# Gathers that keep their running row in two PSUM banks, and one comparison instruction for both one-hot tables of the gate build

## The chip, the cores and the metric

One core of a Trainium2 chip runs the whole program. The metric is the device time of one execution in microseconds (us), the median of three runs. Engines are named as the profile names them: PE (matrix products), PEld (its weight loads), DVE (VectorE), ACT (ScalarE), POOL (GpSimd), SP (the queue that issues most DMA transfers).

## The reference, cut to what matters

One layer: a mixer (an SSD scan and a dilated-window attention), a layer norm, then the PEER feed-forward block, for 1024 prompt tokens and 32 sample tokens of width 1024. Each token picks 128 of 16384 experts (8 heads, 16 each):

```
e = (take(i1, ci // 16) * 128 + take(i2, ci % 16))      # expert numbers
g = softmax(sc)                                         # gates
hid = gelu(einsum('thkd,td->thk', u_tab[e], xb))
out = einsum('thk,thkd->td', g * hid, v_tab[e])
y = layer_norm(ALPHA * h + out)
```

## The kernel before, in words

The prompt's first 512 tokens and the 32 sample tokens are **part 0**, the other 512 tokens **part 1**. Each part runs `first` (attention), `second` (convolutions, then the SSD scan beside the z projections), `third` (output product and norm) and `route` (choice of experts). Then `dense` follows. Stretches are named by these functions below; from 1250 us on all is part 1 or `dense`.

The feed-forward block is computed in two ways. For 608 tokens it is **dense**: all 128x128 experts are multiplied, in 16 chunks `c` of 8 hidden products (weights `in_ut`) and 8 output products (`in_vd`). The hidden rows are weighed with a dense table of gates `g`. For the other 448 tokens, the rows of the chosen experts are **gathered**: an indirect DMA on POOL (L1829) fetches 128 rows of 4 KB, then DVE either multiplies them with the token's row and sums (L1855, table u), or adds them, scaled, to a running sum (L1860, table v). These 896 gathers are a lane of small steps, pumped at a fixed rate per tick beside all other work from part 1's `first` on. The operand that all gathers of a group of tokens share (the token's row `gh`, or the sum `acc`) is in `at`. It lies in SBUF until `dense` sets `self.seat` to two PSUM banks (6 and 7) late in its first chunk; from then on it lies there.

The **gate build** (`gates`, run in ticks beside the first six dense products) makes the table `g`. For each group of four tokens, of which there are 152, it does this: `o2` is where the expert's low number equals a position (DVE, L1603), times the gate (POOL, L1604). `o1` is the same for the high number, in three groups of five on DVE (L1610), in the others on ACT (L1607, L1608). Four fp32 products on PE (L1617) then give the table of four tokens, which ACT moves to SBUF (L1627), and SP to DRAM (`gd`, L1629). Four pairs of buffers (OBUFS) let the comparisons run three groups ahead. `choose` and `experts` prepare the numbers of later tokens in the same ticks.

In `dense`, `product` multiplies one weight tile into a pair of banks (48 matmuls, L427; `double` does two at L1751), and `hidden`, `early` or `output` empty it. Weights `wraw` come in two halves of 256 KB two steps ahead; ACT makes the high part (L368), POOL or DVE the low part (L369). The table `g` is loaded by `table` on SP (L1670), half a chunk (1216 KB, pieces of 512 B) in one DMA.

All engines work their instructions off in program order, and ticks put the lanes' instructions between the matmuls of a product. [...] `proj` takes its output banks from `self.ring` in turn: three banks in part 1's `second`, `third` (last product) and `route`.

Of the kernel before, what the change touches and what calls it, by code (L numbers as in the profile page):

```python
# [7 lines left out]
F32 = mybir.dt.float32  # L8
# [17 lines left out]
NE = 128  # L26
# [25 lines left out]
C_HSEL = C_BM + 8  # L52
C_TSEL = C_HSEL + 8
C_IOTE = C_TSEL + 16
C_NIOTE = C_IOTE + NE
C_PAY = C_NIOTE + NE
C_N = C_PAY + NPAIR


# [5 lines left out]


TPC = [(0, (TE // 32 + 1) // 2 * 32), ((TE // 32 + 1) // 2 * 32, TE // 64 * 32)]

ROWS, LOOK = 6, 5

# [15 lines left out]
NLO = "vpvpvpvp"  # L86


EQ, O1, OBUFS, EARLY = 4, "vavav", 4, [8, 16, 24, 30, 34, 40]


def const_arrays():
# [17 lines left out]
    c[:, C_NIOTE:C_NIOTE + NE] = -np.arange(NE)[None, :]  # L110
    c[:, C_PAY:C_PAY + NPAIR] = (np.arange(NPAIR)[None, :] + 1) * PACK

    def logc(dist):
# [138 lines left out]
class Build:  # L252
# [40 lines left out]
    def run(self):  # L293
# [11 lines left out]
        self.one = cp.tile([128, 1], F32, name="one")  # L305
# [24 lines left out]
    def start(self):  # L330
        nc, t = self.nc, self.t
        load = [(self.cst, t["cst"]), (self.heads, t["heads"].unsqueeze(0).to_broadcast([128, 2, 24])),
                (self.convw, t["convw"]), (self.chans, t["chans"]), (self.keys, t["keys"])]
        self.xrp = self.open("xr", side="right")
        x = self.inputs(0)
        self.load(0, 0)
        next(x)
        self.load(0, 1)
        next(x)
        self.cast(0, 0)  # L340
        self.load(1, 0)
# [12 lines left out]
        nc.vector.memset(self.eps, EPS)  # L354
        nc.vector.memset(self.one, 1.0)
# [457 lines left out]
    def second(self, hf):  # L813

        nc, t, T, PT = self.nc, self.t, self.T, self.PT
        self.ring = [0, 1, 2]
        self.y = self.open(f"y{hf}").tile([128, 12, T], F32, name="y")
        zp, self.zs = self.open(f"z{hf}", 2), 2 if hf else 3
        sp = self.open(f"ss{hf}")
# [329 lines left out]
    def third(self, hf):  # L1149
# [64 lines left out]
        for k, h in WO:  # L1214
            pcs = cuts if (k, 1) in END else self.pcs
            if h == 0:
                b = [[3, 4, 5, 0, 1, 2, 3, 5], [4, 0, 2, 4, 0, 2, 4, 0]][np_ - 1][k]
                acc[k] = [self.P[:, (b + i) % 6, :n] for i, (_, n) in enumerate(pcs)]
            else:
                self.wait(lambda: self.done["mix"])  # L1220
# [328 lines left out]
    def experts(self, sp, table, m, out):  # L1549
# [6 lines left out]
        nc.vector.tensor_single_scalar(ej[:m, 1], ei[:m], NE - 1, op=ALU.bitwise_and)  # L1556
        yield
        nc.vector.tensor_copy(en[:m], ej[:m])
        nc.vector.tensor_scalar_mul(en[:m, 0], en[:m, 0], -1.0)
        yield  # L1560
        tp = self.bank(self.side())
        for k, src in enumerate((en[:m, 0], en[:m, 1], gf[:m])):
# [4 lines left out]
    def gates(self, sp):  # L1567
# [5 lines left out]
        given = 2  # L1573
        groups = [(w, t) for w in range(len(work)) for t in range(work[w][2], work[w][2] + work[w][0], 4)]
        eTs, o12, sts, outs, cp = dict(enumerate(self.given)), {}, {}, {}, {}

        def experts(w):

# [13 lines left out]
        def build(q):  # L1592
            if q >= len(groups):
                return
            w, t0 = groups[q]
            eT = eTs[w]
            o1 = sp.tile([128, 4, 128], F32, name="o1", tag="o1", bufs=OBUFS)
            o2 = sp.tile([128, 4, 128], F32, name="o2", tag="o2", bufs=OBUFS)

            def over(k):  # L1600
                return eT[:, k, t0:t0 + 4].unsqueeze(2).to_broadcast([128, 4, 128])

            nc.vector.tensor_tensor(o2, self.c(C_IOTE).unsqueeze(1).to_broadcast([128, 4, 128]), over(1), op=ALU.is_equal)  # L1603
            nc.gpsimd.tensor_tensor(o2, o2, over(2), op=ALU.mult)  # L1604
            if O1[q % len(O1)] == "a":
                for k in range(4):
                    nc.scalar.activation(o1[:, k], self.c(C_IOTE), AF.Abs, bias=eT[:, 0, t0 + k:t0 + k + 1])  # L1607
                nc.scalar.activation(o1, o1, AF.Relu, scale=-1.0, bias=self.one)  # L1608
            else:
                nc.vector.tensor_tensor(o1, self.c(C_NIOTE).unsqueeze(1).to_broadcast([128, 4, 128]), over(0), op=ALU.is_equal)  # L1610
            o12[q] = o1, o2

        def mults(q):
            o1, o2 = o12.pop(q)
            outs[q] = gp = self.bank(q % 3)
            for k in range(4):
                nc.tensor.matmul(gp[:, k * 128:(k + 1) * 128], o2[:, k], o1[:, k], start=True, stop=True)  # L1617

        def store(q):
            if q < 0:  # L1620
# [28 lines left out]
    def dense(self):  # L1649
# [11 lines left out]
        self.sides = [3]  # L1661

        def table(q):
            if q >= len(steps):
                return
            c, half, k = steps[q]
            if not half and k % 4 == 0:
                gs[c, k // 4] = g = dp.tile([128, n // 32, 4, 32], F32, name="g", tag="g", bufs=2)
                e0 = c * 8 + k
                nc.sync.dma_start(g, self.gd[:, :, e0:e0 + 4, :].rearrange("b j i t -> j b i t"))  # L1670

        def gelu(ge, ps):
            nc.scalar.activation(ge, ps, AF.Gelu)
# [93 lines left out]
        for k in range(8):  # L1767
            if k == len(EARLY):
                self.settle(table_lane)
                self.close("ga", "gc", "best")  # L1770
                dp = self.open("dn", 2)
                for q in range(8):
                    table(q)
            product(4 + k % 2 * 2, hs, EARLY[k] if k < len(EARLY) else DTICKS, lambda ps, k=k: early(k, ps))
        self.settle()
        for k in range(9):
            if k < 8:
# [4 lines left out]
        for q in range(8, 12):  # L1782
            table(q)
        for q, (c, half, k) in enumerate(steps[8:-LASTS], 8):
            table(q + 4)
            if half and k == 0:
                double(q % 3 * 2, (q + 1) % 3 * 2, (ah, al), 2 * DTICKS,
                       [lambda ps, c=c, k=k: output(c, k, ps) for k in range(2)])
            elif not half or k > 1:
                product(q % 3 * 2, (ah, al) if half else hs, DTICKS,  # L1790
                        lambda ps: (output if half else hidden)(c, k, ps))

            self.seat = self.bank(6, 2)

        q0 = self.q
        for i, (s, m) in enumerate(TPC):
            for j, (c, half, k) in enumerate(steps[-LASTS:]):
                ps = self.P[:, i + 2 * j, :m]
# [106 lines left out]
```

## Time and profile before

| | us |
|---|---|
| median of 3 runs | 3946.99 (3944.28 to 3955.53) |
| the profiled execution | 3943.13 |
| its span, first to last instruction | 3940.2 |
| PE busy | 3526.3 (89%) |
| DVE busy | 2826.4 (72%) |
| POOL busy | 2494.5 (63%) |
| ACT busy | 1381.6 (35%) |

The shares are means over stages that differ: the DVE stands near its limit in the middle of the program, PE in the last 1700 us. So the table says how much there is of each engine's work, not where the time is lost; for that the stretches have to be read apart.

### The profile page before, as it was taken

Reading aid. Unit: us, or ns where it says so; the run is one execution under the profiler, and the core shown is the slowest. Engines: PE = TensorE matmul, PEld = TensorE weight load, DVE = VectorE, ACT = ScalarE, POOL = GpSimd, SP = SyncE. Lnnn points to the kernel's source line nnn. Section 1 sums busy time; section 2 is a strip of 40 time slices with the busy share of each in tenths; the row PEclk is TensorE's granted clock in tenths of the full one; section 3 lists DMA queues with packets and bytes.
Section 4 is the critical chain, followed back from the end, with each engine's and each line's share of the span. In section 5 each row is a group of like instructions: output and inputs, shape, how many; then the busy total and the mean of one; then the engine's idle time right before and its main releaser. Section 6 shows DMA issues by size and latency. Waiting matters only on the chain.

```text
span 3940.2 us, 62009 instructions
## 1 busy us (share of the span) xinstructions
PE 3526.3 (89%) x22691; PEld 3178.6 (81%) x22691; DVE 2826.4 (72%) x5547; ACT 1381.6 (35%) x2651; POOL 2494.5 (63%) x2235
## 2 busy tenths in 40 slices
PE   7999898897997887895767999999999999999998
PEld 6757778895765555674666899999999999999997
DVE  2326644488779989899999767667766767776675
ACT  3423324343443333324778222222222222222223
POOL 3204554254747788645788677777767777776774
PEclk9999999998998998897778999999999999999999
DMA  5452235643546457522444789898988999998894
GB/s 159 127 164 74 75 128 199 211 156 107 155 158 212 152 161 249 195 73 78 158 158 185 258 314 324 314 339 316 335 309 318 327 319 339 329 324 304 309 320 154
DMA packets 385521, 875.40 MB, mean 222 GB/s; under 512 B 38976, under 2 KB 149952, under 8 KB 382272
## 3 DMA queue, kind: packets, MB, share of 16 engines
q0 software_dynamic: 129024, 469.82, 33.6%
q1 hardware_dynamic: 256192, 401.63, 30.6%
q8 instruction: 178, 2.92, 0.3%
q14 instruction: 127, 1.04, 0.1%
HBM read 805.40 MB, written 94.65 MB: 228 GB/s over the span
## 4 chain that ended last, share of the span: by engine, by line
PE 38%; DVE 12%; DMA 6%; issue 4%; POOL 3%; ACT 1%; SPq 0%; POOLq 0%; DVEq 0%; ACTq 0%
PE P L427 31%; PE P L1751 5%; DMA wraw<-in_ut 4%; DVE o L1603 2%; DVE acc L1860 2%; DVE o L1610 2%; POOL wlo L369 1%; POOL row L1829 1%; DVE row L1855 1%; POOL o L1604 1%; DMA lng<-in_ln 1%; PE P L1617 1%; DVE mr L1340 0%; PE P L1274 0%; DMA g<-gd 0%
## 5 line engine op out<-in xcount | busy, mean ns | idle before, releaser
L369 POOL TENSOR_TENSOR wlo<-wraw,whi 128x512 fp32r<-128x512 f32 (+1 forms) x621 | 818.2, 1324 | 652.7 <-ACT whi L368 620.5
L368 ACT ACTIVATE whi<-wraw 128x512 fp32r<-128x512 f32 (+1 forms) x820 | 494.8, 625 | 1318.2 <-PE P L427 485.9
L427 PE MATMUL P<-hh,whi 128*128 128x320 f32 (+3 forms) x2648 | 662.5, 315 | 35.9 <-DVE al L1683 27.4
L427 PE MATMUL P<-hh,wlo 128*128 128x320 f32 (+3 forms) x2648 | 655.9, 313 | 17.7 <-DVE wlo L369 9.5
L427 PE MATMUL P<-hl,whi 128*128 128x320 f32 (+3 forms) x2648 | 659.1, 313 | 3.5 <-POOL hl L1295 3.3
L1860 DVE SCALAR_TENSOR_TENSOR P<-row,hid,P 128x1024 f32<-128x1024 f32 x371 | 476.9, 1286 | 57.8 <-DMA row<-in_v,ecol 31.5
L1829 POOL DMA_INDIRECT row<-in_u,ecol x384 | 407.7, 1062 | 152.9 <-DVE row L1855 78.3
L427 PEld LDWEIGHTS P<-hh,whi 128*128 128x128 f32 x2648 | 452.2, 194 | 47.8 <-DVE al L1683 20.8
L427 PEld LDWEIGHTS P<-hh,wlo 128*128 128x128 f32 x2648 | 450.7, 193 | 28.0 <-DVE wlo L369 10.8
L1829 POOL DMA_INDIRECT row<-in_v,ecol x384 | 410.1, 1068 | 90.9 <-issue 71.5
L427 PE MATMUL P<-xh,whi 128*128 128x272 f32 (+4 forms) x1288 | 432.6, 346 | 32.9 <-ACT xh L368 17.3
L427 PEld LDWEIGHTS P<-hl,whi 128*128 128x128 f32 x2648 | 451.5, 193 | 12.8 <-POOL hl L1295 4.7
L1855 DVE SCALAR_TENSOR_TENSOR row<-row,P 128x1024 f32<-128x1024 f32 x320 | 381.8, 1215 | 102.6 <-DMA row<-in_u,ecol 74.0
L427 PE MATMUL P<-xl,whi 128*128 128x272 f32 (+4 forms) x1288 | 420.8, 337 | 7.6 <-POOL xl L369 6.6
L427 PE MATMUL P<-xh,wlo 128*128 128x272 f32 (+4 forms) x1288 | 418.0, 335 | 1.7 <-POOL wlo L369 1.7
L369 DVE TENSOR_TENSOR wlo<-wraw,whi 128x512 fp32r<-128x512 f32 (+1 forms) x199 | 222.7, 1119 | 212.4 <-ACT whi L368 188.3
L427 PE MATMUL P<-ah,wlo 128*128 128x320 f32 (+1 forms) x1536 | 341.9, 302 | 3.1 <-POOL wlo L369 3.1
L427 PE MATMUL P<-ah,whi 128*128 128x320 f32 (+1 forms) x1536 | 342.9, 302 | 0.0
L427 PE MATMUL P<-al,whi 128*128 128x320 f32 (+1 forms) x1536 | 341.4, 301 | 0.0
L1617 PE MATMUL P<-o,o 128*128 128x128 f32 x1216 | 219.2, 338 | 117.1 <-POOL o L1604 99.1
L1617 PEld LDWEIGHTS P<-o,o 128*128 128x128 f32 x1216 | 196.2, 243 | 141.0 <-POOL o L1604 133.6
L427 PEld LDWEIGHTS P<-xh,whi 128*128 128x128 f32 (+1 forms) x1288 | 246.8, 196 | 65.1 <-ACT xh L368 19.1
(393 smaller groups left out, 6794.1 us busy)
## 6 DMA issues: line engine op xcount, KB each, us to landing
wraw<-in_ut SPq DMA_DIRECT2D x256, 256.0 KB
wraw<-in_vd SPq DMA_DIRECT2D x256, 256.0 KB
wraw<-in_wt SPq DMA_DIRECT2D x176, 256.0 KB
gd<-gst SPq DMA_DIRECT2D x19, 2048.0 KB
g<-gd SPq DMA_DIRECT2D x32, 1216.0 KB
wraw<-in_wo SPq DMA_DIRECT2D x64, 256.0 KB
wraw<-in_wq SPq DMA_DIRECT2D x64, 256.0 KB
out_sk<-in_ck SPq DMA_DIRECT2D x8, 2040.0 KB
```

Of the source, the lines that this page charges most:

```text
L368: nc.scalar.activation(hi, src, AF.Copy)
L369: (eng or nc.vector).tensor_tensor(lo, src, hi.bitcast(F32), op=ALU.subtract)
L427: nc.tensor.matmul(outs[i], w[a][:, k, :m], x[b][k][:, s:s + n], start=first and st, stop=last and sp)
L1603: nc.vector.tensor_tensor(o2, self.c(C_IOTE).unsqueeze(1).to_broadcast([128, 4, 128]), over(1), op=ALU.is_equal)
L1604: nc.gpsimd.tensor_tensor(o2, o2, over(2), op=ALU.mult)
L1610: nc.vector.tensor_tensor(o1, self.c(C_NIOTE).unsqueeze(1).to_broadcast([128, 4, 128]), over(0), op=ALU.is_equal)
L1617: nc.tensor.matmul(gp[:, k * 128:(k + 1) * 128], o2[:, k], o1[:, k], start=True, stop=True)
L1751: nc.tensor.matmul(outs[i][j], self.ws[q0 + i][wi][:, e, :], x[xi][e][:, s:s + m], start=e == p == 0, stop=e == last and p == 2)
L1829: nc.gpsimd.indirect_dma_start(out=rows[k], out_offset=None, in_=t["uv"[tab]], in_offset=bass.IndirectOffsetOnAxis(ap=tables(gi)[0][:, s:s ...
L1855: nc.vector.scalar_tensor_tensor(r, r, 1.0, at, op0=ALU.mult, op1=ALU.mult, accum_out=hid[:, s:s + 1])
L1860: nc.vector.scalar_tensor_tensor(at, r, hid[:, s:s + 1], at, op0=ALU.mult, op1=ALU.add)
```

## The change

- From part 1's `second` on, `self.seat` is banks 2 and 3. The row or sum of the gathers moves there at the first gather in `second` and stays. `dense` no longer sets the seat.
- To free these banks, the ring has two banks instead of three, `third` takes its banks from 0, 1, 4 and 5, the dense products use the pairs 0, 4, 6 (`PAIRS`), the gate build's products the banks 0, 1, 7 and its transposes bank 6. The six early products all use pair 4, each emptied (`settle`, two more ticks) before the next.
- In the gate build, a copy of the numbers 0 to 127 (`iota`) is put into bank 6, and one DVE comparison of 1024 elements makes both tables `oo` of a group. ACT's share, the negated numbers and the constants for them go.
- `table` loads half a chunk of `g` in four pieces, one per output product of the chunk before, instead of at once four products ahead.

```diff
     def second(self, hf):
-        self.ring = [0, 1, 2]
+        self.ring = [0, 1] if hf else [0, 1, 2]
+        if hf:
+            self.seat = self.bank(2, 2)
...
-                b = [[3, 4, 5, 0, 1, 2, 3, 5], [4, 0, 2, 4, 0, 2, 4, 0]][np_ - 1][k]
+                b = [[0, 1, 4, 5, 0, 1, 4, 0], [4, 0, 2, 4, 0, 2, 4, 0]][np_ - 1][k]
...
-        nc.vector.tensor_scalar_mul(en[:m, 0], en[:m, 0], -1.0)
...
+        iota = self.bank(6)[:, 384:]
+        nc.scalar.activation(iota, self.c(C_IOTE), AF.Copy)
...
-            nc.vector.tensor_tensor(o2, self.c(C_IOTE).unsqueeze(1).to_broadcast([128, 4, 128]), over(1), op=ALU.is_equal)
-            nc.gpsimd.tensor_tensor(o2, o2, over(2), op=ALU.mult)
-            if O1[q % len(O1)] == "a":
-                for k in range(4):
-                    nc.scalar.activation(o1[:, k], self.c(C_IOTE), AF.Abs, bias=eT[:, 0, t0 + k:t0 + k + 1])
-                nc.scalar.activation(o1, o1, AF.Relu, scale=-1.0, bias=self.one)
-            else:
-                nc.vector.tensor_tensor(o1, self.c(C_NIOTE).unsqueeze(1).to_broadcast([128, 4, 128]), over(0), op=ALU.is_equal)
+            nc.vector.tensor_tensor(oo, iota.unsqueeze(1).unsqueeze(1).to_broadcast([128, 2, 4, 128]),
+                                    eT[:, 0:2, t0:t0 + 4].unsqueeze(3).to_broadcast([128, 2, 4, 128]), op=ALU.is_equal)
+            nc.gpsimd.tensor_tensor(oo[:, 1], oo[:, 1], eT[:, 2, t0:t0 + 4].unsqueeze(2).to_broadcast([128, 4, 128]), op=ALU.mult)
...
-            outs[q] = gp = self.bank(q % 3)
+            outs[q] = gp = self.bank([0, 1, 7][q % 3])
...
-                nc.sync.dma_start(g, self.gd[:, :, e0:e0 + 4, :].rearrange("b j i t -> j b i t"))
+                rows = slice(0, b) if part is None else slice(b * part // 4, b * (part + 1) // 4)
+                nc.sync.dma_start(gs[c, i][:, rows], self.gd[rows, :, e0:e0 + 4, :].rearrange("b j i t -> j b i t"))
...
-            product(4 + k % 2 * 2, hs, EARLY[k] if k < len(EARLY) else DTICKS, lambda ps, k=k: early(k, ps))
+            product(4 if k < len(EARLY) else PAIRS[k % 2 * 2 - 2], hs, EARLY[k] if k < len(EARLY) else DTICKS, lambda ps, k=k: early(k, ps))
+            if k < len(EARLY):
+                self.settle()
...
-            table(q + 4)
+            if half:
+                table(c + 1, k // 4, k % 4)
...
-            self.seat = self.bank(6, 2)
```

The first place is DVE's queue in the gate build, where the numbers of later tokens are prepared between the comparisons (`eT` holds a group's expert numbers, `cst` the constants). Before:

```order
L1603 TENSOR_TENSOR o_16470<-cst,eT 128x512
L1610 TENSOR_TENSOR o_16469<-cst,eT 128x512
L1860 SCALAR_TENSOR_TENSOR acc<-row,hid,acc 128x1024
L1528 CAST cf<-ci 128x256
L1529 CAST sf<-best_13986 128x128
L1530 TENSOR_SCALAR sf<-sf 128x128
L1603 TENSOR_TENSOR o_16489<-cst,eT 128x512
L1610 TENSOR_TENSOR o_16488<-cst,eT 128x512
L1539 TENSOR_TENSOR eq<-sf,cf 128x1024
```

and with the change:

```order
L1602 TENSOR_TENSOR oo<-P,eT 128x1024
L1854 SCALAR_TENSOR_TENSOR P<-row,hid,P 128x1024
L1529 CAST cf<-ci 128x256
L1530 CAST sf<-best_13984 128x128
L1531 TENSOR_SCALAR sf<-sf 128x128
L1602 TENSOR_TENSOR oo<-P,eT 128x1024
L1540 TENSOR_TENSOR eq<-sf,cf 128x1024
```

One instruction that reads PSUM stands where one or two that read SBUF twice stood, and the gather's sum is in `P`, the PSUM tile.

The second place is SP's queue in `dense`. Before, one chunk:

```order
L1670 DMA g<-gd 128x19x128
L395 DMA wraw<-in_ut 128x512 x8
L395 DMA wraw<-in_vd 128x512 x16
L1670 DMA g<-gd 128x19x128
L395 DMA wraw<-in_ut 128x512 x8
L1670 DMA g<-gd 128x19x128
```

and with the change:

```order
L393 DMA wraw<-in_ut 128x512 x10
L393 DMA wraw<-in_vd 128x512 x8
L1664 DMA g<-gd 128x4x128
L393 DMA wraw<-in_vd 128x512 x4
L1664 DMA g<-gd 128x5x128 x2
L393 DMA wraw<-in_vd 128x512 x2
L1664 DMA g<-gd 128x5x128
L393 DMA wraw<-in_vd 128x512 x2
```

The two large loads of a chunk have become eight small ones between the weights of the output products.

## Rows read from the trace of the kernel before

**Rows 1.** Page, part 4: the chain that ended last, by engine and line.
```profile
PE 38%; DVE 12%; DMA 6%; issue 4%; POOL 3%; ACT 1%; SPq 0%; POOLq 0%; DVEq 0%; ACTq 0%
```
**Rows 2.** Windows: us, then PE, PEld, DVE, ACT, POOL busy, clock, DMA share, GB/s.
```profile
1250.00:1540.00 290.00, 221.75 (x1067) 162.87 (x1068) 257.63 (x362) 102.35 (x195) 230.31 (x193) 0.91 0.54 173
1540.00:1660.00 120.00, 99.85 (x487) 83.09 (x485) 108.64 (x101) 35.37 (x64) 84.02 (x64) 0.90 0.69 238
...
1793.00:2172.00 379.00, 261.98 (x1514) 237.19 (x1515) 373.23 (x480) 269.57 (x472) 305.18 (x212) 0.80 0.41 151
...
2216.00:3913.00 1697.00, 1656.08 (x11742) 1651.47 (x11741) 1194.82 (x1482) 449.45 (x753) 1232.67 (x1118) 0.99 0.90 315
```
**Rows 3.** Lines of 1793 to 2172: busy us, mean ns, idle before, releasers.
```profile
L1604 POOL TENSOR_TENSOR o<-o,eT 128x512 f32<-128x512 f32 x152 | 210.6, 1395 | 88.1 <-DVE o L1603 85.3 <-DVE ei L1546 2.4
...
L1603 DVE TENSOR_TENSOR o<-cst,eT 128x512 f32<-128x512 f32 x152 | 151.6, 1019 | 0.8 <-ACT eT L1565 0.8
L1610 DVE TENSOR_TENSOR o<-cst,eT 128x512 f32<-128x512 f32 x91 | 105.5, 1160 | 0.0
...
L1860 DVE SCALAR_TENSOR_TENSOR acc<-row,hid,acc 128x1024 f32<-128x1024 f32 x31 | 67.2, 2167 | 0.0
```
**Rows 4.** Single lines, whole span: ns min/median/max, first and last start.
```profile
L1603 DVE TENSOR_TENSOR o<-cst,eT x152: 674/680/2847, 1793.0 to 2165.5; 128x512 f32<-128x512 f32 x152
L1604 POOL TENSOR_TENSOR o<-o,eT x152: 1032/1421/3162, 1793.8 to 2167.1; 128x512 f32<-128x512 f32 x152
L1860 DVE SCALAR_TENSOR_TENSOR P<-row,hid,P x371: 1273/1289/1292, 2212.7 to 3873.0; 128x1024 f32<-128x1024 f32 x186
L1860 DVE SCALAR_TENSOR_TENSOR acc<-row,hid,acc x77: 1270/2056/3393, 1535.8 to 2207.8; 128x1024 f32<-128x1024 f32 x77
L1677 DVE TENSOR_TENSOR P<-P,g x120: 783/794/800, 2263.4 to 3857.5; 128x608 f32<-128x608 f32 x120
L1855 DVE SCALAR_TENSOR_TENSOR row<-row,P x320: 1200/1216/1224, 2337.9 to 3726.9; 128x1024 f32<-128x1024 f32 x160
```
**Rows 5.** Lines of 1250 to 1540 (first row) and of 1540 to 1660 (second).
```profile
L1855 DVE SCALAR_TENSOR_TENSOR row<-row,gh 128x1024 f32<-128x1024 f32 x68 | 103.3, 1538 | 0.0
...
L1860 DVE SCALAR_TENSOR_TENSOR acc<-row,hid,acc 128x1024 f32<-128x1024 f32 x38 | 68.3, 1797 | 1.0 <-DMA row<-in_v,ecol 0.5
```
**Rows 6.** Timeline of `second`: DVE empties a bank; PE's next projection but one.
```profile
1415.23 0.68 DVE L1116 SCALAR_TENSOR_TENSOR z<-z,P 128x512 f32<-128x512 f32 x1
...
1424.10 0.48 PE L427 MATMUL P<-xh,whi 128*128 128x512 f32 x1
```
**Rows 7.** Chain in order of time: pairs of output products, by start and length.
```profile
2310.11 13.37 PE P L1751 x96
...
2752.37 13.37 PE P L1751 x96
...
2859.33 13.37 PE P L1751 x96
...
2977.67 13.37 PE P L1751 x96
...
3086.63 13.39 PE P L1751 x96
...
3855.20 13.38 PE P L1751 x96
```
**Rows 8.** Timeline of SP and of ACT, 3025 to 3062: start, length, instruction.
```profile
3035.98 0.43 SPq L1670 DMA_DIRECT2D g<-gd  x1
...
3055.73 0.63 ACT L368 ACTIVATE whi<-wraw 128x512 fp32r<-128x512 f32 x1 [11.54 <-DMA wraw<-in_ut]
```
**Rows 9.** A window behind that load, columns as in group 2.
```profile
3050.00:3055.00 5.00, 5.00 (x38) 5.00 (x37) 0.00 (x0) 0.00 (x0) 0.00 (x0) 1.00 1.04 401
```
**Rows 10.** DMA view of 2172 to 3941: queue, packets, MB, share; issues, KB each.
```profile
q1 hardware_dynamic: 153696, 180.78, 31.2%
...
g<-gd SPq DMA_DIRECT2D x32, 1216.0 KB
```

More of the change, by code (lines that the diff above doesn't have):

```diff
@@ L54 @@
 C_IOTE = C_TSEL + 16
-C_NIOTE = C_IOTE + NE
-C_PAY = C_NIOTE + NE
+C_PAY = C_IOTE + NE
 C_N = C_PAY + NPAIR
@@ L67 @@
 TPC = [(0, (TE // 32 + 1) // 2 * 32), ((TE // 32 + 1) // 2 * 32, TE // 64 * 32)]
+PAIRS = [0, 4, 6]
 ROWS, LOOK = 6, 5
@@ L86 @@
 NLO = "vpvpvpvp"
-EQ, O1, OBUFS, EARLY = 4, "vavav", 4, [8, 16, 24, 30, 34, 40]
+EQ, OBUFS, EARLY = 4, 4, [8, 16, 24, 30, 34, 40]
 def const_arrays():
@@ L109, in const_arrays @@
     c[:, C_IOTE:C_IOTE + NE] = np.arange(NE)[None, :]
-    c[:, C_NIOTE:C_NIOTE + NE] = -np.arange(NE)[None, :]
     c[:, C_PAY:C_PAY + NPAIR] = (np.arange(NPAIR)[None, :] + 1) * PACK
@@ L304, in run @@
         self.eps = cp.tile([128, 1], F32, name="eps")
-        self.one = cp.tile([128, 1], F32, name="one")
         self.ctail = cp.tile([128, 20, 3], F32, name="ctail")
@@ L354, in start @@
         nc.vector.memset(self.eps, EPS)
-        nc.vector.memset(self.one, 1.0)
         nc.vector.memset(self.ctail, 0.0)
@@ L1596, in build @@
             eT = eTs[w]
[L1597 to L1601, printed above, removed]
-            nc.vector.tensor_tensor(o2, self.c(C_IOTE).unsqueeze(1).to_broadcast([128, 4, 128]), over(1), op=ALU.is_equal)
-            nc.gpsimd.tensor_tensor(o2, o2, over(2), op=ALU.mult)
-            if O1[q % len(O1)] == "a":
-                for k in range(4):
-                    nc.scalar.activation(o1[:, k], self.c(C_IOTE), AF.Abs, bias=eT[:, 0, t0 + k:t0 + k + 1])
-                nc.scalar.activation(o1, o1, AF.Relu, scale=-1.0, bias=self.one)
-            else:
-                nc.vector.tensor_tensor(o1, self.c(C_NIOTE).unsqueeze(1).to_broadcast([128, 4, 128]), over(0), op=ALU.is_equal)
-            o12[q] = o1, o2
+            oo = sp.tile([128, 2, 4, 128], F32, name="oo", tag="oo", bufs=OBUFS)
+            nc.vector.tensor_tensor(oo, iota.unsqueeze(1).unsqueeze(1).to_broadcast([128, 2, 4, 128]),
+                                    eT[:, 0:2, t0:t0 + 4].unsqueeze(3).to_broadcast([128, 2, 4, 128]), op=ALU.is_equal)
+            nc.gpsimd.tensor_tensor(oo[:, 1], oo[:, 1], eT[:, 2, t0:t0 + 4].unsqueeze(2).to_broadcast([128, 4, 128]), op=ALU.mult)
+            o12[q] = oo
         def mults(q):
-            o1, o2 = o12.pop(q)
-            outs[q] = gp = self.bank(q % 3)
+            oo = o12.pop(q)
+            outs[q] = gp = self.bank([0, 1, 7][q % 3])
             for k in range(4):
-                nc.tensor.matmul(gp[:, k * 128:(k + 1) * 128], o2[:, k], o1[:, k], start=True, stop=True)
+                nc.tensor.matmul(gp[:, k * 128:(k + 1) * 128], oo[:, 1, k], oo[:, 0, k], start=True, stop=True)
         def store(q):
@@ L1660, in dense, with table @@
         self.turns = LO5
[L1661 to L1669, printed above, removed]
-                nc.sync.dma_start(g, self.gd[:, :, e0:e0 + 4, :].rearrange("b j i t -> j b i t"))
+        self.sides = [6]
+        def table(c, i, part=None):
+            if c < NE // 8:
+                if not part:
+                    gs[c, i] = dp.tile([128, n // 32, 4, 32], F32, name="g", tag="g", bufs=2)
+                b, e0 = n // 32, c * 8 + i * 4
+                rows = slice(0, b) if part is None else slice(b * part // 4, b * (part + 1) // 4)
+                nc.sync.dma_start(gs[c, i][:, rows], self.gd[rows, :, e0:e0 + 4, :].rearrange("b j i t -> j b i t"))
         def gelu(ge, ps):
@@ L1771, in dense @@
                 dp = self.open("dn", 2)
-                for q in range(8):
-                    table(q)
-            product(4 + k % 2 * 2, hs, EARLY[k] if k < len(EARLY) else DTICKS, lambda ps, k=k: early(k, ps))
+                for i in range(2):
+                    table(0, i)
+            product(4 if k < len(EARLY) else PAIRS[k % 2 * 2 - 2], hs, EARLY[k] if k < len(EARLY) else DTICKS, lambda ps, k=k: early(k, ps))
+            if k < len(EARLY):
+                self.settle()
         self.settle()
@@ L1781, in dense @@
         self.pumping.rate = self.left / ((len(steps) - 8) * DTICKS - 20)
-        for q in range(8, 12):
-            table(q)
         for q, (c, half, k) in enumerate(steps[8:-LASTS], 8):
-            table(q + 4)
+            if half:
+                table(c + 1, k // 4, k % 4)
             if half and k == 0:
-                double(q % 3 * 2, (q + 1) % 3 * 2, (ah, al), 2 * DTICKS,
+                double(PAIRS[q % 3], PAIRS[(q + 1) % 3], (ah, al), 2 * DTICKS,
                        [lambda ps, c=c, k=k: output(c, k, ps) for k in range(2)])
             elif not half or k > 1:
-                product(q % 3 * 2, (ah, al) if half else hs, DTICKS,
+                product(PAIRS[q % 3], (ah, al) if half else hs, DTICKS,
                         lambda ps: (output if half else hidden)(c, k, ps))
-            self.seat = self.bank(6, 2)
         q0 = self.q
@@ L1797, in dense @@
             for j, (c, half, k) in enumerate(steps[-LASTS:]):
-                ps = self.P[:, i + 2 * j, :m]
+                ps = self.P[:, PAIRS[j] + i, :m]
                 self.step((ah, al), [ps], [(s, m)], DTICKS, q=q0 + j, ahead=not i)
```

## Prediction

> **What bounds the kernel now.** I read the chain of waits first: PE carries 38% of it and DVE 12% [rows 1], so the limit changes along the program. The windows by stage say where [rows 2]. In the gate build (1793 to 2172) DVE is busy 373 of 379 us, PE 262 at a mean granted clock of 0.80, POOL 305. That stage is as long as DVE's queue. In `second` and `third` of part 1 DVE is busy 258 of 290 and 109 of 120 us, with PE at 222 and 100: DVE first, PE close behind in `third`. From 2216 on PE is busy 1656 of 1697 us; only the missing 41 us can be had there, and the DMA engines are busy 0.90 of that time.
>
> The third view, single lines with their least and greatest durations, shows why DVE is slow in the middle [rows 4]. The same scaled add L1860 on 1024 elements takes 1273 to 1292 ns in all 371 cases with its sum in PSUM, but 1270 to 3393 ns, median 2056, with the sum in SBUF. POOL works beside both (73% of the late stretch, 80% of the gate build). So an instruction that reads SBUF twice is held up by POOL, one that reads SBUF once is not; L1677 (783 to 800 ns) and L1855 with PSUM (1200 to 1224) agree. POOL is held up in turn: its multiply L1604 takes 1032 ns at best and 1421 at the median. L1603, 680 ns when alone, has a mean of 1019 [rows 3].
>
> **The change, part by part.** All is set against the profiled execution: 3943.1 us, span 3940.2, with 2.9 us around it, 0.1% below the median of 3946.99.
>
> *Gate build.* DVE loses L1603 (151.6 us), L1610 (105.5 us) and the slow form of 31 gathers (67.2 us) [rows 3]. What else it does there is 373.2 - 151.6 - 105.5 - 67.2 = 49 us. It gains 152 comparisons of 1024 elements with one operand in PSUM and one in SBUF. The trace has no such instruction; the nearest rows are L1855 with PSUM, the same length at 1216 ns, and L1677, the same kind of operation on 608 elements in 794 ns; the two lie about 1 ns an element apart (422 ns for 416), so length sets the time [rows 4]. I take 1.22. So 152 x 1.22 = 185 us, 33 gathers (31, and two more in the 12 added ticks at 0.2 each) x 1.29 = 43 us, the rest 49: DVE needs 277 us. ACT loses its two tables in five and is no limit. POOL keeps its 152 multiplies, but beside a comparison that leaves it alone each should come near its 1032 ns: 305 falls towards 250. PE needs its 262 us unless the clock rises. With DVE at 277 and PE at 262, in one chain of queues worked off in order, gaps of some 13 us are likely: I take 290, that is **-89 us**. Ends: 262, if PE's work alone decides (-117); 335, if POOL keeps its 305 us and gaps of a tenth (-44).
>
> The early products now share one pair of banks, so PE waits for ACT's emptying (L1673) between products. Two ticks lie between, with two groups' products on PE and over 3 us of DVE work; I cost it at nothing. Without that cover it would be under 1 us at each of five places. The copy of `iota` is one short ACT instruction before the first group.
>
> *Part 1.* `second` has 68 gathers in its window at 1538 ns against 1216 with PSUM [rows 4, 5]: 68 x 0.32 = 22 us of DVE, and 15 more stand before 1250, about 5 us. 45 of the 128 come before the switch and stay. `third` has 38 at 1797 against 1289: 19 us. DVE is not the only limit. In `third` PE idles for just 20 us [rows 2], so I take 10 (ends 0 and 20). In `second` I take 18 (ends 0 and 35, since POOL is also held up less). Together **-28 us**. The seat's copies on ACT are as many as before, only earlier.
>
> The ring of two banks costs nothing if a bank is empty before the next projection but one. The timeline shows DVE reading a projection's bank at 1415.23, done 0.7 us later, and the next projection but one starting at 1424.10 [rows 6]: 8 us to spare. That cover is DVE's promptness. If it goes, PE waits for DVE and whatever DVE has queued before, a gather's row among it.
>
> *Dense products.* A chunk of sixteen products with nothing in its way takes 2859.33 - 2752.37 = 106.96 us [rows 7]. From 2310.11 to 3855.20 lie 14 chunks: 1545.1 - 14 x 106.96 = 48 us of delay. The worst take 11 to 14 us each (2859.33 to 2977.67 is 118.3), three of them, where a group of gathers ends and its norm runs; the change leaves these. The others, about 11 us in all, fall behind a `g` load: it is issued at 3035.98, the weight behind it lets ACT start only at 3055.73 [rows 8], with the DMA engines full at 401 GB/s meanwhile [rows 9], and that chunk is 2.0 us long over [rows 7]. Four pieces with weights between them should remove most of that and a little of the bad three: **-12 us** (ends 0 and -30). On SP there are 90 more issues of 0.43 us [rows 8], 39 us of a queue that mostly waits for free weight buffers: nothing. Fewer gathers are left for `dense` by two or three of some 690: nothing.
>
> [...]
>
> Sum: 89 + 28 + 12 = 129, so 3943.1 - 129 = **3814 us**.
>
> **Rivals.**
>
> *The gate build stays with POOL and the hand-overs.* POOL's idle time before L1604 is now put down to DVE, 85 us [rows 3], which speaks against it; that PE waits for POOL's multiply, a step later in each group, speaks for it. With 335 us there: 3943 - 44 - 28 - 12 = 3859.
>
> *Two banks are too few in part 1.* 24 + 16 + 15 projections use the ring or the closer banks. Half a microsecond of waiting at each eats the 28 us, and the time is 3843. For: DVE is over 89% busy there. Against: the 8 us of [rows 6].
>
> *Small pieces are dear.* Queue q1 needs 0.312 of 1769 us for 180.8 MB [rows 10], 3.05 us a MB, so a `g` tile of 1.25 MB costs 3.8 us and 30 of them 114 us. If pieces cost twice that, 114 us must fit into the 170 us in which the DMA engines now idle; if half of it shows, 3943 - 89 - 28 + 57 = 3883. Against: the packets of 512 B are the same ones, and transfers of 256 KB already run at 401 GB/s in sum [rows 9].
>
> *The other side: the long comparison is held up by POOL after all.* It still reads numbers from SBUF and writes 4 KB a partition there. If POOL held it to double, 2.44 us, DVE would need 152 x 2.44 + 43 + 49 = 463 us, about 470 with gaps, 91 more than now: 3943 + 91 - 28 - 12 = 3994, slower. It decides from a mean of about 1.95 us on. Against it stands that none of 811 instructions with one operand in PSUM was held up [rows 4].
>
> **How the numbers follow.** I give the forecast 0.80, the POOL-bound gate build 0.10, the two banks 0.05, the dear pieces 0.03, the held-up comparison 0.02. The ends of all terms together would be 3741 and 3899; they will not all fall to one side. The range, 3768 to 3862, takes in the first two rivals and leaves the last two out. A difference under 0.3% (12 us) can't be told from none: all but the last rival are faster by more. Faster 0.96, same 0.02, slower 0.02.
>
> **What would show it.** In the profile after: the comparison near 1.22 us with hardly any spread, the gate build some 290 us long with L1604 nearer 1.05 than 1.4 us, PE's granted clock there perhaps above 0.80; gathers at 1.22 and 1.29 us from `second` on; no long wait of a projection for DVE's reading of a bank; chunks of 107 us except at the ends of three groups. It is wrong if the comparison spreads like L1603 did, if the gate build stays above 335 us, or if chunks get longer than they were.

## The result and the profile after

The changed kernel takes **3777.93 us** (median of 4 runs, 3775.33 to 3780.7), the kernel before 3945.64 us on the same chip: ratio 0.9574, 95% interval 0.955 to 0.9599. The forecast was 3814 us, in a range of 3768 to 3862. So the direction and the range hold, and the kernel is 36 us faster than forecast.

The two profiled spans are 3940.2 and 3778.1 us, 162.1 apart. Five marks divide the difference (us from the start of the span); four are the last instruction of their kind in a stage, the third is the first of its kind. The last one is the last matmul that reads `al`:

| mark | before | after | stage's gain | forecast |
|---|---|---|---|---|
| last tanh of z, end of `second` | 1508.4 | 1488.2 | 20 | 18 |
| last norm product of `third` | 1653.5 | 1620.5 | 13 | 10 |
| first comparison of the gate build | 1793.0 | 1760.3 | 0 | 0 |
| last gate product (L1617, now L1611) | 2170.8 | 2049.3 | 88.8 | 89 |
| last paired output product (L1751, now L1745) | 3868.0 | 3707.2 | **39.3** | **12** |

About 1 us more goes behind the last mark. Four of the terms came out within 3 us; the fifth is more than three times its size.

The page of the changed kernel, busy times and the chain that ended last, answers to the table of before and to [rows 1]:

```profile
PE 3475.6 (92%) x22691; PEld 3142.5 (83%) x22691; DVE 2684.3 (71%) x5449; ACT 1285.9 (34%) x2347; POOL 2370.2 (63%) x2235
...
PE 45%; DVE 8%; issue 4%; POOL 3%; DMA 2%; ACT 1%; DVEq 0%; POOLq 0%; SPq 0%; ACTq 0%
```

DVE's share of the chain fell from 12% to 8% and that of DMA from 6% to 2%. The second fall is the one that the forecast did not see coming.

The windows of the changed kernel, one for each stage (`second`, `third`, gate build, dense products), with the columns of [rows 2]:

```profile
1201.00:1489.00 288.00, 233.98 (x1145) 174.36 (x1143) 259.44 (x398) 102.72 (x201) 214.23 (x210) 0.93 0.58 187
1489.00:1621.00 132.00, 114.79 (x532) 93.89 (x533) 108.69 (x112) 48.52 (x82) 91.17 (x80) 0.88 0.74 267
1760.00:2051.00 291.00, 222.01 (x1510) 206.15 (x1510) 275.98 (x389) 172.69 (x176) 229.81 (x214) 0.88 0.54 196
...
2049.00:3707.00 1658.00, 1643.81 (x11725) 1641.12 (x11725) 1198.51 (x1483) 458.32 (x761) 1231.44 (x1120) 1.00 0.93 327
```

In the gate build DVE is busy 276 us (forecast 277) of 291 (forecast 290). POOL fell from 305 to 230 though it does the same multiplies, and PE from 262 to 222 at nearly the same number of matmuls: its mean granted clock rose from 0.80 to 0.88 while its idle time in the stage fell from 117 to 69 us. In the dense products PE now lacks only 14 us of 1658, where it lacked 41 of 1697 [rows 2].

Single lines of the changed kernel, with the columns of [rows 4]:

```profile
L1602 DVE TENSOR_TENSOR oo<-P,eT x152: 1205/1212/1226, 1760.3 to 2045.8; 128x1024 f32<-128x1024 f32 x152
...
L1604 POOL TENSOR_TENSOR oo<-oo,eT x152: 1028/1041/1952, 1761.5 to 2047.1; 128x512 f32<-128x512 f32 x152
...
L1849 DVE SCALAR_TENSOR_TENSOR row<-row,P x403: 1202/1214/1223, 1202.6 to 3563.9; 128x1024 f32<-128x1024 f32 x135
...
L1854 DVE SCALAR_TENSOR_TENSOR P<-row,hid,P x448: 1272/1283/1291, 1514.8 to 3712.3; 128x1024 f32<-128x1024 f32 x150
```

1003 DVE instructions with one operand in PSUM, and not one was held up; the longest comparison took 1226 ns (forecast 1.22 us with hardly any spread). POOL's multiply L1604 has a median of 1041 ns instead of 1421 [rows 4].

The dense products are another matter. The chain of the changed kernel in order of time, a pair of output products per chunk, as in [rows 7]:

```profile
2721.89 13.39 PE P L1745 x96
...
2829.13 13.38 PE P L1745 x96
...
2936.33 13.38 PE P L1745 x96
...
3365.28 13.37 PE P L1745 x96
...
3411.82 7.96 DMA lng<-in_ln
...
3479.93 13.39 PE P L1745 x96
```

From 2292.87 on, every chunk takes 107.2 us (2721.89 to 2829.13), except one at the end of a group of gathers, where the norm's weights `lng` are loaded: 3365.28 to 3479.93 is 114.65 us. The forecast left three chunks of 11 to 14 us over, those in which a group ends. In the change the groups end at 2204.7, 2807.2 and 3411.8 (where `lng` is loaded). The second of these chunks loses nothing, the third 7.4 us, and the first, which lies ahead of 2292.87 and takes 109.2 us, loses 2.0.

### The profile page after: what moved, and what is told of

It is laid out like the page before. It is cut to its first block, busy times and chain, and to the rows that moved or that the text cites. A ratio compares the mean times of both kernels' runs of the same rounds, so it can differ in the third digit from the quotient of the medians.

```text
span 3778.1 us, 61732 instructions
## 1 busy us (share of the span) xinstructions
PE 3475.6 (92%) x22691; PEld 3142.5 (83%) x22691; DVE 2684.3 (71%) x5449; ACT 1285.9 (34%) x2347; POOL 2370.2 (63%) x2235
## 4 chain that ended last, share of the span: by engine, by line
PE 45%; DVE 8%; issue 4%; POOL 3%; DMA 2%; ACT 1%; DVEq 0%; POOLq 0%; SPq 0%; ACTq 0%
PE P L425 38%; PE P L1745 5%; DVE oo L1602 2%; POOL oo L1604 1%; DMA row<-in_v,ecol 1%; PE P L1611 1%; DVE P L1854 1%; POOL row L1823 1%; POOL wlo L367 1%; DVE mr L1341 0%; POOL eq L1542 0%; PE P L1275 0%; DMA lng<-in_ln 0%; DVE keys L1345 0%; DVE keys L1339 0%
## 5 line engine op out<-in xcount | busy, mean ns | idle before, releaser
L367 POOL TENSOR_TENSOR wlo<-wraw,whi 128x512 fp32r<-128x512 f32 (+1 forms) x621 | 807.0, 1305 | 604.0 <-ACT whi L366 548.7
L425 PE MATMUL P<-hh,whi 128*128 128x320 f32 (+3 forms) x2648 | 654.6, 312 | 7.5 <-ACT hh L1304 4.6
L425 PE MATMUL P<-hh,wlo 128*128 128x320 f32 (+3 forms) x2648 | 647.7, 310 | 4.8 <-POOL wlo L367 4.5
L1854 DVE SCALAR_TENSOR_TENSOR P<-row,hid,P 128x1024 f32<-128x1024 f32 x448 | 575.3, 1284 | 28.7 <-DMA row<-in_v,ecol 14.7
L1849 DVE SCALAR_TENSOR_TENSOR row<-row,P 128x1024 f32<-128x1024 f32 x403 | 478.4, 1213 | 62.8 <-DMA row<-in_u,ecol 25.9
L1823 POOL DMA_INDIRECT row<-in_u,ecol x384 | 389.1, 1013 | 155.4 <-DVE row L1849 79.4
L425 PEld LDWEIGHTS P<-hl,whi 128*128 128x128 f32 x2648 | 445.2, 191 | 13.1 <-POOL hl L1296 4.7
L425 PEld LDWEIGHTS P<-hh,wlo 128*128 128x128 f32 x2648 | 444.8, 191 | 13.1 <-POOL wlo L367 4.7
L1823 POOL DMA_INDIRECT row<-in_v,ecol x384 | 378.7, 986 | 101.7 <-issue 49.2
L367 DVE TENSOR_TENSOR wlo<-wraw,whi 128x512 fp32r<-128x512 f32 (+1 forms) x199 | 212.6, 1069 | 211.1 <-ACT whi L366 202.3
L425 PEld LDWEIGHTS P<-xl,whi 128*128 128x128 f32 (+1 forms) x1288 | 247.6, 196 | 35.0 <-POOL xl L367 8.2
L425 PEld LDWEIGHTS P<-xh,wlo 128*128 128x128 f32 (+1 forms) x1288 | 247.2, 196 | 25.4 <-issue 4.2
```

The source lines that it names most:

```text
L367: (eng or nc.vector).tensor_tensor(lo, src, hi.bitcast(F32), op=ALU.subtract)
L425: nc.tensor.matmul(outs[i], w[a][:, k, :m], x[b][k][:, s:s + n], start=first and st, stop=last and sp)
L1823: nc.gpsimd.indirect_dma_start(out=rows[k], out_offset=None, in_=t["uv"[tab]], in_offset=bass.IndirectOffsetOnAxis(ap=tables(gi)[0][:, s:s ...
L1849: nc.vector.scalar_tensor_tensor(r, r, 1.0, at, op0=ALU.mult, op1=ALU.mult, accum_out=hid[:, s:s + 1])
L1854: nc.vector.scalar_tensor_tensor(at, r, hid[:, s:s + 1], at, op0=ALU.mult, op1=ALU.add)
```

## The experiments

Two questions were open: whether the gains in the middle come from the PSUM operand, as argued, and what gave 39 us in the dense products where 12 were expected. "Dense time" below runs from the last gate product to the last paired output product: 1697.2 us before, 1657.9 in the change.

### Whole loads of g at their old places, the rest of the change kept

```diff
-            if half:
-                table(c + 1, k // 4, k % 4)
+            table(q + 4)
```

(with `table` as in the kernel before)

> The change, but with the gate table loaded half a chunk in one DMA, four products ahead, as before. Theory A (the pieces saved the time in the dense products): from the second chunk's to the last chunk's pair of output products it takes 1535 to 1550 us again instead of 1511, and the whole is 25 to 40 us longer than the change, 3803 to 3818 us. Theory B (the pieces do nothing; the gathers' group ends merely fall at other places in the chunks now): 1511 us there, and within 6 us of 3778.

3826.21 us (3816.15 to 3831.84), ratio to before 0.9696 [0.9654, 0.9738]: 48 us slower than the change, where 25 to 40 were expected. The dense time is 1704.1 us, 46 more. PE's waits from 2040 to 3760 in this kernel (us in total, times, longest):

```profile
PE P L425 <- DVE al L1677: 28.4, 11, 6.7
PE P L425 <- POOL wlo L367: 9.2, 2, 6.5
```

The long line, PE waiting for DVE to empty a pair of banks, is that of the kernel before, and not there in the change:

```profile
PE P L427 <- DVE al L1683: 27.4, 8, 6.1
PE P L427 <- POOL wlo L369: 8.4, 4, 4.7
```

(before, 2172 to 3870) and

```profile
PE P L425 <- POOL wlo L367: 6.2, 2, 4.5
```

(change, 2049 to 3707). So the whole gain of the dense products, and some us more, hangs on how `g` is loaded.

### The pieces alone, in the kernel before

```diff
-            table(q + 4)
+            if half:
+                table(c + 1, k // 4, k % 4)
```

(with `table` as in the change)

> The kernel before, with nothing but the gate table's loads cut into four pieces, one per output product of the chunk before. Theory A (the pieces save the time): everything up to the dense products as before, 1545 us from the second to the last pair falls to 1510 to 1520, the whole 25 to 40 us below before, 3905 to 3920 us. Theory B (the place of the group ends in the chunks decides): 1545 us stays, the whole within 8 us of before.

3897.37 us (3892.06 to 3901.49), ratio 0.9879 [0.9839, 0.9919]. The dense time is 1651.6 us, 46 less than before; again more than expected. Alone or undone, the pieces are worth 46 us, so the other parts of the change gave nothing in this stage. In fact they cost some 6 us there (1657.9 against 1651.6), 4 of them because every chunk is 107.24 us long instead of 106.95.

Where the 46 us lay can be read from the starts of the pairs: 27 us of them in the three chunks with a group's end (37.0 us over before, 10.4 with the pieces), 11 in the other chunks that the forecast counted, and 8 ahead of 2310.11, where its sum of 48 us begins (139.3 us from the last gate product to there, 131.4 with the pieces).

### How an early load reaches PE

The timeline of the kernel before shows it, in the chunk that the forecast quoted as a "worst" one (start, length, instruction, in brackets the idle time before it and what ended it):

```profile
2916.01 0.43 SPq L1670 DMA_DIRECT2D g<-gd  x1
...
2937.26 0.63 ACT L368 ACTIVATE whi<-wraw 128x512 fp32r<-128x512 f32 x1 [14.21 <-DMA wraw<-in_ut]
...
2937.80 0.66 ACT L1673 ACTIVATE P<-P 128x608 f32<-128x608 f32 x1
...
2938.49 0.80 DVE L1677 TENSOR_TENSOR P<-P,g 128x608 f32<-128x608 f32 x1 [10.26 <-ACT P L1673]
...
2941.23 0.54 PE L427 MATMUL P<-hh,whi 128*128 128x320 f32 x2 [1.71 <-DVE al L1683]
```

1216 KB of `g` are issued ahead of the weights of a hidden product. The weights come late, and ACT waits 14.2 us to convert them. The gelu of a product that PE had finished stands behind that cast on ACT; DVE's work on it waits 10.3 us for the gelu, and PE for the banks that DVE then empties. The name that PE's wait bears, `DVE al`, is the last link of a chain that begins with a DMA.

This chunk is 11.4 us over, and the wait shown is only 1.7 of them. Two more waits follow at its norm:

```profile
2954.31 0.90 SPq L1884 DMA_DIRECT2D lng<-in_ln  x2
...
2961.50 4.80 POOL L1885 TENSOR_TENSOR acc<-acc,lng 128x1024 f32<-128x1024 f32 x2 [6.60 <-DMA lng<-in_ln]
...
2964.52 0.84 PE L427 MATMUL P<-hh,whi 128*128 128x320 f32 x2 [2.96 <-DVE al L1683]
...
2968.77 0.88 PE L427 MATMUL P<-hh,wlo 128*128 128x320 f32 x2 [2.90 <-POOL wlo L369]
```

The third wait stands behind POOL's two steps with the norm's weights, for which POOL itself waited 6.6 us. The three waits make 7.6 us. The other 3.8 us are matmuls that run slower behind them. Windows of this stretch, columns of [rows 2]:

```profile
2960.00:2964.00 4.00, 1.57 (x12) 1.32 (x10) 2.34 (x4) 3.18 (x5) 2.42 (x2) 1.00 0.39 155
2964.00:2968.00 4.00, 1.35 (x4) 1.00 (x4) 3.37 (x6) 0.64 (x3) 3.83 (x3) 0.51 0.21 87
2968.00:2972.00 4.00, 3.23 (x13) 3.23 (x14) 2.87 (x5) 0.60 (x2) 3.67 (x4) 0.50 0.86 278
...
2976.00:2980.00 4.00, 4.00 (x30) 4.00 (x30) 3.26 (x6) 1.70 (x3) 3.38 (x4) 1.00 1.06 370
```

After the wait of 2.96 us PE's granted clock stands at 0.51 and 0.50 (the trace's clock records hold two levels, 0.50 and 1.00), and a pair of matmuls takes 0.71 us instead of 0.44; in the window from 2976 on it is back at 1.00. Over the whole stage it is alike: of the 46 us that the pieces alone win, 31 are PE's waits (43.8 us became 12.4), and 14 are PE's busy time for the same matmuls (1653.7 us became 1639.5).

ACT's waits for weights over the dense products show how late these were, first of the kernel before:

```profile
ACT whi L368 <- DMA wraw<-in_ut: 427.2, 67, 20.0
...
ACT whi L368 <- DMA wraw<-in_vd: 49.9, 18, 8.8
```

and of the change:

```profile
ACT whi L366 <- DMA wraw<-in_ut: 120.9, 38, 13.9
...
ACT whi L366 <- DMA wraw<-in_vd: 91.0, 31, 6.8
```

Together 477 us of late weights became 212: those for the hidden products fell by 306 us, those for the output products rose by 41.

### Place or size of the load

Whole loads at the first and fifth output product of the chunk before:

```diff
-            if half:
-                table(c + 1, k // 4, k % 4)
+            if half and k % 4 == 0:
+                table(c + 1, k // 4)
```

> The change, but each half chunk of the gate table is loaded in one DMA, at the first and the fifth output product of the chunk before, so whole but earlier than before. Theory A (it is the spreading: a DMA of 1216 KB ahead of the weights makes these late wherever it stands): from the last product of the gate build to the last pair of output products about 1700 us, as with the whole loads at their old places (1704), the whole near 3820 us. Theory C (it is the place: the second load stood just ahead of a chunk's first hidden products, whose weighing the engines wait for): near 1658 us as in the change, the whole within 8 us of 3778.

3793.82 us (3785.2 to 3797.69), ratio 0.9605 [0.9588, 0.9622]; dense time 1671.1, between the two expectations.

Four pieces, back to back, at the old places:

```diff
-                nc.sync.dma_start(g, self.gd[:, :, e0:e0 + 4, :].rearrange("b j i t -> j b i t"))
+                for part in range(4):
+                    rows = slice(n // 32 * part // 4, n // 32 * (part + 1) // 4)
+                    nc.sync.dma_start(g[:, rows], self.gd[rows, :, e0:e0 + 4, :].rearrange("b j i t -> j b i t"))
```

(against the first experiment's kernel)

> The change, but the four pieces of half a chunk are issued one behind the other at the two old places. Theory A (spreading): as late as the whole load, near 1700 us in the dense products, the whole 3810 to 3830 us. Theory D (a small DMA is passed by others more easily, cutting alone is enough): near 1658 us, the whole within 8 us of 3778. Theory C (place): near 1700 us too, so this run tells D from the other two.

3809.14 us (3805.43 to 3812.05), ratio 0.964 [0.9622, 0.9657]; dense time 1690.3, nearer to that of whole loads. Its wait of PE, from 2047 to 3715, beside the 28.4 us of whole loads there:

```profile
PE P L425 <- DVE al L1679: 15.7, 6, 5.2
```

Against whole loads at the old places (1704.1), the place alone gives 33 us, the cutting alone 14, both together 46; by the medians of the whole kernel it is 32, 17 and 48. Each dense time comes from one execution, and a kernel with whole loads can vary by 34 us (the one with two banks below), so a few us of these shares are uncertain. The place counts most. In the kernel with whole early loads PE's wait for `DVE al` at a hidden product is gone, though the weights are no less late in sum. ACT's waits for them there, from 2042 to 3713:

```profile
ACT whi L366 <- DMA wraw<-in_ut: 309.0, 75, 16.1
...
ACT whi L366 <- DMA wraw<-in_vd: 134.4, 43, 14.9
```

Together they are 443 us; with whole loads at the old places it was 438 (395.1 and 43.2, from 2047 to 3715). So it is not the sum of the late weights that costs PE its time, but where they fall. Banks of an output product are emptied by DVE without ACT, which would explain it; no run tests that alone.

### Is it the order on ACT, or the weights themselves

In the first experiment's kernel, the cast of the next weights is issued behind the first tick of a product, so that the gelu of the product before stands ahead of it (`late` is set at the start of the dense products):

```diff
-        if ahead:
+        if ahead and not self.late:
             self.cast(q + 2, 0)
...
                 self.tick()
+                if ahead and self.late and j + 1 == cuts[0]:
+                    self.cast(q + 2, 0)
```

(and the same in `double`)

> The change with whole loads at their old places (the first run) and one more edit: in the dense products ACT's cast of the weights for two products ahead is issued behind the first tick of a product instead of ahead of it, so that the gelu of the product before stands in front of it in ACT's queue. Theory E (a late weight holds up ACT, the gelu stands behind it, the pair of banks comes free late, and PE waits for that): the dense products fall from 1704 us to 1670 to 1690, PE's wait for the low part of the weighed rows (20.6 us) to under 8, the whole 3790 to 3815 us. Rival F (PE lacks the weight itself): dense products and whole within 5 us of the first run, 3826.

3812.37 us (3808.27 to 3816.0), ratio 0.9648 [0.9618, 0.9677]; dense time 1696.0, only 8 less than in the first experiment (14 less by the medians, which come from two chips) and not the 1670 to 1690 expected. PE's waits from 2040 to 3745:

```profile
PE P L425 <- POOL wlo L367: 18.6, 7, 8.3
PE P L425 <- ACT whi L366: 7.5, 3, 4.0
...
PE P L425 <- DVE al L1679: 3.3, 2, 2.9
```

The wait for the banks fell from 28.4 to 3.3 us (under 8 was expected), as the chain above says, but waits for the weights rose from 9.2 to 26.1, 18.6 of them for the low part. So the order on ACT is the way the delay took, and not its cause: with it mended, PE waits for the late weights directly.

### The comparison from SBUF

```diff
-        iota = self.bank(6)[:, 384:]
-        nc.scalar.activation(iota, self.c(C_IOTE), AF.Copy)
+        iota = self.c(C_IOTE)
```

> The change, but the one comparison of 1024 elements reads the numbers 0 to 127 from SBUF instead of PSUM. Theory A (an instruction that reads SBUF twice is held up by POOL): the comparison's least time stays near 1.21 us, its mean rises to 1.7 to 2.4 us and POOL's multiply to about 1.4; the gate build takes 350 to 420 us instead of 290, the whole 3838 to 3908 us. Theory B (the gate build gained because one instruction took the place of two and ACT's share went): mean near 1.22 us, and within 6 us of 3778.

3864.66 us (3863.34 to 3869.32), ratio 0.98 [0.9761, 0.9839], 87 us slower than the change. The last gate product comes at 2130.8 instead of 2049.3. The same two instructions, single lines as above:

```profile
L1601 DVE TENSOR_TENSOR oo<-cst,eT x152: 1206/1862/3652, 1757.2 to 2126.5; 128x1024 f32<-128x1024 f32 x152
...
L1603 POOL TENSOR_TENSOR oo<-oo,eT x152: 1029/1164/3024, 1758.6 to 2128.6; 128x512 f32<-128x512 f32 x152
```

At its best the comparison is as short from SBUF as from PSUM (1206 and 1205 ns), so where the operand lies costs or saves nothing by itself. Beside POOL it is 1862 at the median, against 1212. The timeline shows that it is POOL: of 132 comparisons from SBUF whose times it gives one by one, the 20 beside which POOL ran no arithmetic instruction took 1.21 to 1.22 us, also where POOL issued a gather meanwhile; every longer one, up to 3.65 us, ran beside one. In the kernel before it is alike: of the comparisons of 512 elements in its gate build that the timeline gives one by one (in windows of 5 us), the 51 beside no arithmetic of POOL took 0.67 to 0.69 us, the 125 beside it 1.52 us at the median and up to 4.26. One instruction instead of two, without the copy in PSUM, wins little: from first comparison to last gate product it is 373.6 us, before 377.8, in the change 289.0.

### The gathers' operand late in PSUM

```diff
-        if hf:
-            self.seat = self.bank(2, 2)
...
+            self.seat = self.bank(2, 2)
```

(removed from `second`, put back late in the first chunk of `dense`)

> The change, but the gathers' row or sum stays in SBUF until late in the first dense chunk, as before. Theory A (held up by POOL in SBUF): second is about 20 us longer, third about 13, the gate build 10 to 30 (33 gathers at 2.1 instead of 1.28 us), the dense products the same; the whole 3815 to 3840 us. Theory B (the gain in part 1 came from the other banks of the output product and from the order): second and third as in the change, the whole within 8 us of 3778.

3838.15 us (3835.91 to 3841.43), ratio 0.9731 [0.9693, 0.977], 60 us slower than the change. `second` ends at 1507.2 (19 us later), `third` 13 us more, the gate build takes 312 us instead of 289. That is the whole gain of part 1, and 23 us of the gate build's.

### Two banks in the ring, in the kernel before

```diff
-        self.ring = [0, 1, 2]
+        self.ring = [0, 1] if hf else [0, 1, 2]
```

> The kernel before, with the ring of two banks instead of three in the second part and nothing else changed. Theory A (a bank is emptied some 8 us before its next use): second, third and route end within 2 us of before, the whole within 8 us of before. Rival (PE waits for DVE's reading of a bank): half a microsecond or more at each of some 40 projections, 20 us or more longer.

3945.0 us (3928.43 to 3962.42, 10 runs), ratio 0.999 [0.997, 1.001]. No cost shows in the time, and the rival's 28 us are ruled out. A little is to be seen in the profile: `second` ends 2.6 us later (1511.0), and two waits of PE for DVE's reading of a projection (2.3 us in all) are new; in the change there are two such waits, of 4.1 and 1.9 us. The closer banks of `third` were not tested alone; one wait there is for DVE's reading of a bank (1.7 us).

### Further along the same way

In the changed gate build DVE is still the fullest engine and ACT has room. In one group of six ACT makes the table of the high number:

```diff
+            if q % 6 == 3:
+                nc.vector.tensor_tensor(oo[:, 1], iota.unsqueeze(1).to_broadcast([128, 4, 128]),
+                                        eT[:, 1, t0:t0 + 4].unsqueeze(2).to_broadcast([128, 4, 128]), op=ALU.is_equal)
+                for k in range(4):
+                    nc.scalar.activation(oo[:, 0, k], self.c(C_IOTE), AF.Abs, scale=-1.0, bias=eT[:, 0, t0 + k:t0 + k + 1])
+                nc.scalar.activation(oo[:, 0], oo[:, 0], AF.Relu, scale=-1.0, bias=self.c(C_ONE, 1))
+            else:
```

> The change, but in one group of six the high table is made by ACT (as before the change, without the negated numbers) and DVE compares 512 elements in place of 1024. Theory A (the gate build is as long as DVE's queue): 25 groups x 0.53 us = 13 us less for DVE, the gate build 8 to 13 us shorter, the whole 3765 to 3772 us. Rival (PE and the hand-overs set it now): gate build and whole within 3 us of the change.

3766.61 us (3765.98 to 3771.0), ratio 0.9536 [0.9519, 0.9553]; the last gate product at 2034.7, 14.6 us earlier.

With it, the late cast of above:

```diff
+        self.late = True
```

> The change with ACT's share of one group in six and the later cast. If the three thirds of the gain add up, the gate build is as with the share alone and the dense products 1650 to 1658 us instead of 1660: 3757 to 3767 us. Rival (the later cast makes POOL's low parts late and PE waits for these instead): 3770 us or more.

3769.9 us (3767.1 to 3776.86), ratio 0.954 [0.9512, 0.9568]: no gain, and close to the rival's 3770. That fits: with the pieces in place there is little left for it to mend.

With ACT's share, half as many gathers per tick in the gate build (they run later, where DVE has room):

```diff
-GATHER = [2.5, 3.2, 3, 0.0, 0.2]
+GATHER = [2.5, 3.2, 3, 0.0, 0.1]
```

> The change with ACT's share of one group in six and half as many gathers in the gate build (0.1 per tick). Theory A (the gate build is as long as DVE's queue, and the dense products have room): 16 gathers x 1.28 us = 21 us less for DVE, the gate build 10 to 20 us shorter, the dense products the same: 3748 to 3758 us. Rival (in the dense products 16 more gathers of 0.5 MB meet DMA engines that are busy 0.92 of the time): those get 10 us or more longer and the whole stays at 3767 or above.

3748.17 us (3745.28 to 3750.35), ratio 0.9487 [0.9459, 0.9516]; the last gate product at 2021.6, another 13.1 us earlier.

And none (`0.0` in the same place):

> The run before (ACT's share of one group in six), with no gathers at all in the gate build. Theory A (still DVE's queue): DVE falls from 239 to about 218 us, PE stays near 214, the gate build takes 245 to 255 us instead of 263, the dense products with 33 more gathers than the change as long as before; the whole 3732 to 3742 us. Rival (PE and the hand-overs, or the DMA engines in the dense products, take over): the whole 3745 us or more.

**3743.07 us** (3739.99 to 3743.66), ratio 0.9476 [0.946, 0.9493], the best version here, 35 us below the change. The step gave 5 us; the time lies between the two expectations. Its gate build and its dense products, columns as above:

```profile
1762.00:2015.00 253.00, 203.59 (x1494) 189.62 (x1495) 220.83 (x352) 203.25 (x295) 198.59 (x181) 0.93 0.40 163
2015.00:3671.00 1656.00, 1645.10 (x11728) 1642.34 (x11727) 1237.78 (x1515) 460.98 (x761) 1261.81 (x1150) 1.00 0.95 336
```

DVE is no longer the limit there (221 of 253 us, PE, ACT and POOL each near 200). And the dense products take the moved gathers in at no cost that shows (1656 us), with the DMA engines at a share of 0.95.

## Why the prediction was right, and where it was not

**What bounds the kernel** was read rightly for the middle: DVE, lengthened by two operands in SBUF beside POOL. The comparison from SBUF and the late seat give back 81.5 and 54 us of what the forecast put down to it. The comparison's times, 1206 to 3652 ns from SBUF and 1205 to 1226 from PSUM, agree.

**Gate build**, -89 forecast, -88.8 measured. The busy time of DVE was right to 1 us, the gaps too. PE's 262 us were taken as a floor "unless the clock rises"; it rose, and PE needed 222, so that end (-117) was no floor.

**Part 1**, -28 forecast, -33 measured, both parts near their middle values; undoing the seat takes 19 and 13 us back.

**Dense products**, -12 forecast, -39 measured, past the end of -30. The step that failed is this one: "The worst take 11 to 14 us each [...], three of them, where a group of gathers ends and its norm runs; the change leaves these." The norm does run in those chunks. But a `g` load stands near each norm (38 us or less between its issue and that of `lng`), and behind these loads ACT waits 20.0, 14.2 and 11.0 us for weights. So the one had used up part of the lead of two products, by which weights run ahead, when the other came; this is read from the timeline of the one chunk above, and not tested for the two others. Neither makes 11 us by itself: every chunk of before has two such loads, and seven of the fourteen lose nothing, and with the loads spread, the three norms cost 2.0, 0 and 7.4 us in the change (5.1, 0 and 5.3 with the pieces alone). The forecast gave each delay to the event next to it in time, which made 11 us of what was 46; of the rest, 27 us lay in those three chunks and 8 ahead of its sum. The timeline from `g` over ACT, DVE and PE was in the trace of before; it was followed only for one load, among the mildest (2.0 us).

A premise failed beside it: "only the missing 41 us can be had there" (43.8 between the marks used here). The pieces alone won 46, because PE's matmuls too had been longer behind the waits, at a granted clock of 0.50.

**The rivals.** The gate build did not stay with POOL (291 us instead of 335). Two banks are enough (0.999; by the terms of the sum the time that goes with that rival is 3842, not 3843). The long comparison was not held up; read from SBUF it would have been, at a median of 1862 ns, and even then the gate build was not longer than before. By the terms of that rival the gate build is as long as the old 379 us at a mean of 1.89 us, not 1.95; from SBUF it was 1.74. Pieces are not dear: with them the DMA share rose from 0.90 to 0.93 while the time fell, and with whole loads the dense products are 46 us longer.

**The forecast as a whole** held because its largest term was worked out from rows of the same kind of instruction in both forms, and because its range reached 46 us below the forecast, more than the 27 us by which the dense term was off. Had the gate build or part 1 come out at its better end as well (28 or 22 us less), the time would have left the range; to that extent it is luck.

## What to carry to other kernels

An operand that many DVE instructions share was worth a place in PSUM here, where POOL worked beside them: 87 us for the comparison's, 60 for the gathers'. Look for one line whose times spread in SBUF and not in PSUM, as 1206 to 3652 against 1205 to 1226 ns. When a long stage loses time in bursts, follow each burst back through the queues to its first late event before saying which bursts a change will leave; delays that draw on the same lookahead need not add up event by event (two loads without a norm cost nothing in seven chunks here, the norms with the loads spread 2.0, 0 and 7.4 us, the chunks with both 11 to 14), and a wait of PE can cost more than its length where the granted clock falls with it (7.6 us of waits went with 11.4 us of delay, at a clock of 0.50). A bulk load belongs where what is queued behind it isn't needed soon; here an earlier place was worth 33 us and the cutting alone 14.

## What the runs showed of the hardware beyond that

PE's mean granted clock in the gate build went 0.80, 0.88 and 0.93 in the kernel before, the change and the best version, while its idle time in the stage fell from 117 to 69 and 49 us; the matmuls there took 262, 222 and 204 us. No run separates which of the shorter waits brought how much of this.

A chunk without delays takes 107.24 us in every kernel with the new bank pairs (0, 4, 6) and 106.95 in those without (the kernel before, that with the pieces alone, that with two banks in the ring). The 0.29 us per chunk make 4 us in all. No run tells whether the banks or something else that goes with them cause it; this stays open.
